# Seven block products instead of eight in one row unit of every chunk pair of w_out, gate/up and w_down

## The chip, the cores and the metric

One core of a Trainium2 chip runs the whole program in one launch. The metric is the device time of a run in microseconds (us), lower is better. The kernel before takes 2527.98 us (median of 3 runs, 2527.86 to 2528.4).

## What is computed

A decoder trunk of two layers on x of 256 positions by 2048 channels, in float32. The parts of a layer that matter here:

```python
h = rms_norm(x, mix_norm[l])
proj = h @ w_in[l]                          # q, k, v, u/v of the spatial unit, two gates
branch_a = attention(q, k, v) @ w_attn_branch[l]
branch_b = spatial_unit(u, v) @ w_sgu_branch[l]
merged = sigmoid(ga) * branch_a + sigmoid(gb) * branch_b
x = x + merged @ w_out[l]                   # 2048 x 2048
h2 = rms_norm(x, ffn_norm[l])
x = x + (silu(h2 @ w_gate[l]) * (h2 @ w_up[l])) @ w_down[l]   # FF = 5632
```

## The kernel before

All weights stream through once. A weight is cut into **chunks** of 512 columns, and a chunk into **halves** of 256 rows. `Stream` handles halves in the order of use: a DMA on SP's queue brings a half of 128x(2x512) to `raw` (L117, 512 KB, 4 buffers); ScalarE copies it to `whi` in the type fp32r (L130) and VectorE writes the rest, raw minus whi, to `wlo` (L131). Three pairs of whi and wlo exist (pool `wsp`), and `next()` asks for the split of the half that lies two ahead (`W_SPLIT` = 3), so a copy into whi waits until TensorE is done with the half three places earlier.

The activations lie transposed in **units** of 512 channels (four slices of 128), also as a high part uh and a low part ul. `product` multiplies all units with one chunk into two PSUM banks, one for each block t of 128 positions. Each half costs 2 (t) x 2 (slices of 128 rows) x 3 matmuls: uh by whi (L204), uh by wlo (L205), ul by whi (L206). That is 12 matmuls of 128x128 by 128x512 per half. After each half `tick()` issues steps that were put off with `after(n, ...)`.

In the feed-forward part each f of 11 has a gate chunk and an up chunk. After the gate product ScalarE takes tanh of both banks (L706) and VectorE multiplies (L707); after the up product VectorE finishes `hid` (L711). `transposed` then turns hid: two VectorE transposes into `box` (L218), 16 DMAs of 32 KB on SP's queue to `tt` (L222), and a split into uh and ul (L241, L242). When all 11 units of hT stand, `residual` multiplies them with the four chunks of w_down and adds each product to xs (L642); w_out goes through the same function.

TensorE's instructions run in the order in which they are written. The order on the other engines is fixed when the program is built, by a scheduler. Four PSUM banks (`ps_acc`) hold products, so two products are open at a time.

Of the kernel before, what the change touches and what calls it, by code (L numbers as in the profile page):

```python
# [8 lines left out]
F32 = mybir.dt.float32  # L9
# [5 lines left out]
P = 128  # L15
# [14 lines left out]
EPS = 1e-6  # L30
B = 32
W_LOAD = 5
W_SPLIT = 3
N_WARM = 8
TT = 1
# [12 lines left out]
def hybrid_trunk(ctx: ExitStack, tc: tile.TileContext, x, mix_norm, w_in, q_norm, k_norm, sinks,  # L48
# [16 lines left out]
    uid = [0]  # L65

    def nm(s):
        uid[0] += 1
        return f"{s}_{uid[0]}"

    def slot(shape, dt=F32, name="s"):
        return big.tile(shape, dt, tag="s4", name=nm(name))

    def temp(shape=(P, CW), name="t"):
        return tmp.tile(list(shape), F32, tag="t2", name=nm(name))

    def tiny(n, name, bufs=None):
        return small.tile([P, n], F32, tag=f"{name}{n}", name=nm(name), bufs=bufs)
# [7 lines left out]
    chunks = []  # L86
    for l in range(DEPTH):
        wl = w_in[l]
        for kind, c in FIRST_PART:
            o = {"kv": O_KV, "q": 0, "v": O_V, "u": O_U, "gate": O_GATE}[kind] + c * CW  # L90
            chunks.append(wl[:, o:o + CW])
        chunks += cols_of(w_attn_branch[l], NCH)
        for j in range(NCH):
            chunks.append(wl[:, O_GATE + D + j * CW:O_GATE + D + (j + 1) * CW])
            chunks.append(w_sgu_branch[l, :, j * CW:(j + 1) * CW])
        chunks += cols_of(w_out[l], NCH)
        for f in range(NF):
            chunks.append(w_gate[l, :, f * CW:(f + 1) * CW])
            chunks.append(w_up[l, :, f * CW:(f + 1) * CW])
        chunks += cols_of(w_down[l], NCH)  # L100
    halves = [(w, h) for w in chunks for h in range(w.shape[0] // (2 * P))]

    class Stream:

        def __init__(self):
            self.raws, self.parts = [], []
            self.at = 0

        def load(self, upto):
            while len(self.raws) < min(upto, len(halves)):
                w, h = halves[len(self.raws)]
                raw = wraw.tile([P, 2, CW], F32, tag="raw", name=nm("raw"))
                src = w[2 * h * P:2 * (h + 1) * P, :].rearrange("(k p) n -> p k n", p=P)
                if self.raws:
                    self.loaded = nc.sync.dma_start(raw, src)  # L117
                else:
                    for i in range(2):
                        self.loaded = nc.sync.dma_start(raw[:, i:i + 1], src[:, i:i + 1])  # L120
                self.raws.append(raw)

        def split(self, upto):
            while len(self.parts) < min(upto, len(halves)):
                raw = self.raws[len(self.parts)]
                hi = wsp.tile([P, 2, CW], F32R, tag="hi", name=nm("whi"))
                lo = wsp.tile([P, 2, CW], F32R, tag="lo", name=nm("wlo"))
                one = len(self.parts) < 2
                for i in ([slice(0, 1), slice(1, 2)] if one else [slice(0, 2)]):
                    nc.scalar.activation(hi[:, i, :], raw[:, i, :], AF.Copy)  # L130
                    self.last = nc.vector.tensor_tensor(out=lo[:, i, :], in0=raw[:, i, :], in1=hi[:, i, :].bitcast(F32),  # L131
                                            op=ALU.subtract)
                self.parts.append((hi, lo))
# [13 lines left out]
    def after(n, fn):  # L147
        steps.append((slot_no[0] + n, fn))
# [39 lines left out]
    def rsqrt(dst, src, n):  # L188
        nc.gpsimd.tensor_tensor(out=dst, in0=src, in1=neg_half[:, :n], op=ALU.pow)  # L189

    def product(units):

        ps = [ps_acc.tile([P, CW], F32, tag="acc", name=nm("acc")) for _ in range(NT)]
        n = 2 * len(units)
        for h in range(n):
            hi, lo = stream.next()
            uh, ul = units[h // 2]
            for t in range(NT):
                for kk in range(2):
                    k = 2 * (h % 2) + kk  # L200
                    a, b = uh[:, k, t * P:(t + 1) * P], ul[:, k, t * P:(t + 1) * P]
                    first = h == 0 and kk == 0
                    last = h == n - 1 and kk == 1
                    nc.tensor.matmul(ps[t], a, hi[:, kk, :], start=first, stop=False)  # L204
                    nc.tensor.matmul(ps[t], a, lo[:, kk, :], start=False, stop=False)  # L205
                    nc.tensor.matmul(ps[t], b, hi[:, kk, :], start=False, stop=last)  # L206
            if h < n - 1:
                tick()
        return ps

    def turn(dst, src, per=1):

# [13 lines left out]
        for j in range(4):  # L226
            after(1 + j // per, lambda j=j: move(j))

    def transposed(units, c, src, cols=None, on_pe=False):

        uh = slot([P, 4, S], F32R, "uh")
        ul = slot([P, 4, S], F32R, "ul")
# [29 lines left out]
            return  # L262

        tt = slot([P, 4, 4, NT, B], name="tt")

        def blocks_of(k0):
            return lambda k, step: tt[:, :, k0 + k:k0 + k + step].rearrange("p i k t r -> p (k t) i r")

        def done():
            parts(2, 2, blocks_of(2))  # L270
            units[c] = (uh, ul)

        turn(tt, src)
        after(6, lambda: parts(0, 2, blocks_of(0)))
        after(7, done)

    class Norm:


        def __init__(self, cols):  # L280
            self.cols = cols
            self.ss = [tiny(NCH, f"ss{t}", 2) for t in range(NT)]
            self.units = [None] * NCH

# [5 lines left out]

        def unit(self, c, on_pe=False):
            transposed(self.units, c, xs[:, :, c * CW:(c + 1) * CW], cols=self.cols[:, 4 * c:4 * c + 4],
                       on_pe=on_pe)

        def finish(self):
            self.r, self.rh, self.rr = [], [], []
# [332 lines left out]
        tick()  # L629
        return dst  # L630

    def residual(units, cols, scale=1.0):

        nxt = Norm(cols) if cols is not None else None
        for j in range(NCH):
            ps = product(units)
            for t in range(NT):
                n = 1 if cols is not None or j < NCH - 1 else 2
                w = CW // n
                for i in range(n):  # L640
                    sl = slice(j * CW + i * w, j * CW + (i + 1) * w)
                    nc.vector.scalar_tensor_tensor(out=xs[:, t, sl], in0=ps[t][:, i * w:(i + 1) * w], scalar=scale,  # L642
                                                   in1=xs[:, t, sl], op0=ALU.mult, op1=ALU.add)
                    if cols is None:
                        eng = nc.sync if i == 0 else nc.scalar
                        eng.dma_start(out[0, t * P:(t + 1) * P, sl], xs[:, t, sl])
            if cols is not None:
                after(2, lambda j=j: nxt.unit(j, j == NCH - 1))
                after(3, lambda j=j: nxt.squares(j))
                if j == NCH - 1:  # L650
                    after(4, lambda: nxt.finish())
            tick()
        return nxt

    prepare(0)
# [1 line left out]
    for l in range(DEPTH):  # L657
# [27 lines left out]
        for j in range(NCH):  # L685
            gb = gate(norm.units)
            ps = product(spa.sguT)
            for t in range(NT):
                nc.vector.scalar_tensor_tensor(out=gb[:, t, :], in0=gb[:, t, :], scalar=1.0, in1=ps[t],
                                               op0=ALU.add, op1=ALU.mult)  # L690
                nc.vector.tensor_tensor(out=ga[j][:, t, :], in0=ga[j][:, t, :], in1=gb[:, t, :], op=ALU.add)
            after(2, lambda j=j: transposed(mT, j, ga[j], on_pe=j == NCH - 1))
            tick()

        norm = residual(mT, ffn_cols(l), scale=0.5)


        if l + 1 < DEPTH:
            after(20, lambda: prepare(l + 1))
        hT = [None] * NF  # L700
        for f in range(NF):
            ps = product(norm.units)
            a = slot([P, NT, CW], name="hid")
            for t in range(NT):
                th = a[:, t, :]
                nc.scalar.activation(th, ps[t], AF.Tanh, scale=norm.rh[t])  # L706
                nc.vector.scalar_tensor_tensor(out=th, in0=th, scalar=1.0, in1=ps[t], op0=ALU.add, op1=ALU.mult)  # L707
            tick()
            ps = product(norm.units)
            for t in range(NT):  # L710
                nc.vector.scalar_tensor_tensor(out=a[:, t, :], in0=ps[t], scalar=norm.rr[t], in1=a[:, t, :],  # L711
                                               op0=ALU.mult, op1=ALU.mult)
            after(2, lambda f=f, a=a: transposed(hT, f, a))
            tick()
        norm = residual(hT, mix_cols(l + 1) if l + 1 < DEPTH else None)


# [35 lines left out]
```

## Time and profile before

| | |
|---|---|
| median of 3 runs | 2527.98 us |
| the profiled execution, its own time | 2530.42 us |
| its span, first to last instruction | 2528.7 us |
| halves, matmuls of halves | 896, 3 x 3584 |
| TensorE / VectorE / ScalarE busy | 99% / 59% / 45% |
| mean granted TensorE clock | 0.999 |

Lines of the profile name engine, source line and tile. PE is TensorE (PEld its weight loads), DVE VectorE, ACT ScalarE, SPq the DMA queue of SP. A matmul's row shows when it starts; its length of 0.39 us includes the time until its last result is out, so the next one starts before it ends.

### The profile page before, as it was taken

The page shows a single profiled execution, that of the slowest core. Times are in us where ns is not written, and L with a number is a line of the kernel's source. Part 1 is how long each engine was busy: PE and PEld are TensorE (multiplying, and loading weights), DVE is VectorE, ACT ScalarE, POOL GpSimd, SP SyncE. Part 2 cuts the span into 40 slices and gives each one's busy share as a digit, 9 for nine tenths or more (in the row PEclk, how much of TensorE's full clock was granted, in tenths as well). Part 3 has the DMA queues.
Part 4 walks back from the last instruction along what each step waited for, and adds up shares of the span by engine and source line. Part 5 has one row for each costly group of instructions (what it writes and reads, how often), then busy time and mean ns, then how long its engine had stood idle before and what let it go on. Part 6 is the DMA issues. An engine that isn't in the chain of part 4 may idle for free.

```text
span 2528.7 us, 30796 instructions
## 1 busy us (share of the span) xinstructions
PE 2515.7 (99%) x11306; PEld 2078.0 (82%) x11306; DVE 1490.8 (59%) x1817; ACT 1145.8 (45%) x1394; POOL 44.9 (2%) x51
## 2 busy tenths in 40 slices
PE   9999999999999999999999999999999999999999
PEld 7788888878888888888888888888888888888887
DVE  7786555565555555555567865556655555555444
ACT  5455444454444444444445554444444444444333
POOL 1100000000000000000000000000000000000000
PEclk9999999999999999999999999999999999999999
DMA  7656666666666666666666556666666666676665
GB/s 233 212 163 187 200 188 210 202 219 202 199 211 203 203 209 202 210 201 203 203 173 219 151 166 216 201 209 202 207 205 201 209 192 222 189 220 201 203 203 158
DMA packets 287816, 506.18 MB, mean 200 GB/s; under 512 B 28016, under 2 KB 55760, under 8 KB 287664
## 3 DMA queue, kind: packets, MB, share of 16 engines
q1 hardware_dynamic: 286544, 502.12, 64.4%
q0 software_dynamic: 800, 1.83, 0.4%
q8 instruction: 88, 1.44, 0.2%
q14 instruction: 64, 0.52, 0.1%
q10 hardware_dynamic: 320, 0.27, 0.0%
HBM read 475.27 MB, written 2.10 MB: 189 GB/s over the span
## 4 chain that ended last, share of the span: by engine, by line
PE 93%; DMA 3%; SPq 2%; DVE 1%; ACT 1%; issue 1%; POOL 0%; DVEq 0%; ACTq 0%
PE acc L205 30%; PE acc L206 30%; PE acc L204 30%; SPq L222 2%; DMA raw<-in_w_out_dram 1%; DVE wlo L131 1%; PE po L551 1%; ACT whi L130 1%; PE psc L512 1%; DMA raw<-in_w_in_dram 1%; PE ppt L541 0%; DMA raw<-in_w_down_dram 0%; DMA raw<-in_w_gate_dram 0%; PE pt L259 0%; PE psg L615 0%
## 5 line engine op out<-in xcount | busy, mean ns | idle before, releaser
L131 DVE TENSOR_TENSOR wlo<-raw,whi 128x1024 fp32r<-128x1024 f32 (+1 forms) x898 | 1094.3, 1221 | 990.2 <-ACT whi L130 982.8
L130 ACT ACTIVATE whi<-raw 128x1024 fp32r<-128x1024 f32 (+1 forms) x898 | 949.3, 1058 | 1323.2 <-PE acc L206 1078.5
L204 PE MATMUL acc<-whi,uh 128*128 128x512 f32 x3584 | 1401.2, 391 | 2.4 <-ACT whi L130 1.7
L205 PE MATMUL acc<-wlo,uh 128*128 128x512 f32 x3584 | 1396.8, 390 | 5.8 <-DVE wlo L131 5.8
L206 PE MATMUL acc<-whi,ul 128*128 128x512 f32 x3584 | 1396.0, 390 | 0.0
L205 PEld LDWEIGHTS acc<-wlo,uh 128*128 128x128 f32 x3584 | 673.3, 188 | 149.5 <-DVE wlo L131 11.2
L204 PEld LDWEIGHTS acc<-whi,uh 128*128 128x128 f32 x3584 | 673.2, 188 | 142.5 <-ACT whi L130 2.7
L206 PEld LDWEIGHTS acc<-whi,ul 128*128 128x128 f32 x3584 | 673.1, 188 | 140.0 <-DVE ul L250 0.2
L242 DVE TENSOR_TENSOR ul<-tt,uh 128x512 fp32r<-128x512 f32 x72 | 49.2, 684 | 0.0
L241 ACT ACTIVATE uh<-tt 128x512 fp32r<-128x512 f32 x72 | 40.9, 616 | 5.3 <-DMA tt<-box 5.3
L218 DVE STREAM_TRANSPOSE box<-hid 128x512 f32<-128x512 f32 x44 | 30.9, 703 | 0.0
L711 DVE SCALAR_TENSOR_TENSOR hid<-acc,rr,hid 128x512 f32<-128x512 f32 x44 | 30.9, 743 | 0.0
L529 ACT ACTIVATE pr<-pr,negm 128x128 f32<-128x128 f32 (+1 forms) x64 | 28.3, 444 | 5.3 <-DVE negm L522 5.3
L706 ACT ACTIVATE hid<-acc,rhalf 128x512 f32<-128x512 f32 x44 | 27.9, 678 | 3.2 <-PE acc L206 1.9
L707 DVE SCALAR_TENSOR_TENSOR hid<-hid,acc 128x512 f32<-128x512 f32 x44 | 28.3, 680 | 1.1 <-ACT hid L706 1.1
L551 PEld LDWEIGHTS po<-kv,pT 128*128 128x128 f32 x192 | 23.9, 191 | 1.2
L189 POOL TENSOR_TENSOR rstd<-var,neg_half 128x1 f32<-128x1 f32 x8 | 4.4, 557 | 1120.8 <-DVE var L300 1120.8
L516 DVE TENSOR_TENSOR pr<-psc,mask 128x256 f32<-128x256 f32 (+1 forms) x32 | 17.1, 550 | 11.8 <-PE psc L512 11.8
L642 DVE SCALAR_TENSOR_TENSOR xs<-acc,xs 128x512 f32<-128x512 f32 (+1 forms) x34 | 21.0, 650 | 5.1 <-PE acc L206 5.1
L628 ACT ACTIVATE gate<-acc,rhalf 128x512 f32<-128x512 f32 x32 | 21.0, 681 | 6.4 <-PE acc L206 6.4
L551 PE MATMUL po<-kv,pT 128*128 128x64 f32 x192 | 23.1, 270 | 0.0
L288 ACT ACTIVATE junk<-xs 128x512 f32<-128x512 f32 x32 | 19.9, 624 | 6.8 <-DVE xs L642 5.3
(111 smaller groups left out, 502.4 us busy)
## 6 DMA issues: line engine op xcount, KB each, us to landing
raw<-in_w_in_dram SPq DMA_DIRECT2D x239, 512.0 KB, 4.0
raw<-in_w_gate_dram SPq DMA_DIRECT2D x176, 512.0 KB, 4.3
raw<-in_w_up_dram SPq DMA_DIRECT2D x176, 512.0 KB, 4.4
raw<-in_w_down_dram SPq DMA_DIRECT2D x176, 512.0 KB, 4.2
raw<-in_w_out_dram SPq DMA_DIRECT2D x64, 512.0 KB, 4.2
tt<-box SPq DMA_DIRECT2D x784, 32.0 KB, 2.7
raw<-in_w_attn_branch_dram SPq DMA_DIRECT2D x32, 512.0 KB, 4.6
raw<-in_w_sgu_branch_dram SPq DMA_DIRECT2D x32, 512.0 KB, 4.7
```

The lines of the kernel that those rows point to most:

```text
L130: nc.scalar.activation(hi[:, i, :], raw[:, i, :], AF.Copy)
L131: self.last = nc.vector.tensor_tensor(out=lo[:, i, :], in0=raw[:, i, :], in1=hi[:, i, :].bitcast(F32), op=ALU.subtract)
L204: nc.tensor.matmul(ps[t], a, hi[:, kk, :], start=first, stop=False)
L205: nc.tensor.matmul(ps[t], a, lo[:, kk, :], start=False, stop=False)
L206: nc.tensor.matmul(ps[t], b, hi[:, kk, :], start=False, stop=last)
L218: nc.vector.transpose(box[:, :, :, t, :].rearrange("p j k r -> p k j r"), iv[:, t])
L222: nc.sync.dma_start(dst[j * B:(j + 1) * B, i], box[i * B:(i + 1) * B, j])
L241: nc.scalar.activation(h, s_, AF.Copy)
L242: nc.vector.tensor_tensor(out=l, in0=s_, in1=h.bitcast(F32), op=ALU.subtract)
L529: nc.scalar.activation(pr4[:, h, :nk], pr4[:, h, :nk], AF.Exp, bias=nm_[:, h:h + 1], accum_out=den[:, h:h + 1])
L551: nc.tensor.matmul(po[:, h, :], pT[kb][:, h, :], self.kv[:, kb, KVW + g * HD:KVW + (g + 1) * HD], start=kb == 0, stop=kb == t)
L711: nc.vector.scalar_tensor_tensor(out=a[:, t, :], in0=ps[t], scalar=norm.rr[t], in1=a[:, t, :], op0=ALU.mult, op1=ALU.mult)
```

## The change

Two chunks (w_out 0 and 1, 2 and 3; gate and up of one f; w_down likewise) become a **pair** that is multiplied together into four banks: a[0], a[1] for the first chunk, b[0], b[1] for the second. In row unit 0 of the pair (two halves of each chunk) the product of 2 position blocks by 2 halves by 2 chunks is done in seven products of 6 matmuls, in Strassen's way (Winograd's form), and not in eight. The other units are done as before, in 12 matmuls per half (tags G for the first chunk, U for the second).

```diff
-    big = ctx.enter_context(tc.tile_pool(name="big", bufs=29))
-    wraw = ctx.enter_context(tc.tile_pool(name="wraw", bufs=4))
+    big = ctx.enter_context(tc.tile_pool(name="big", bufs=24))
+    wraw = ctx.enter_context(tc.tile_pool(name="wraw", bufs=7))
...
+        return [dict(tag="P1", loads=[(k11, wa, h1)], src=k11),
+                dict(tag="P5", loads=[(k12, wb, h1)], sum=(k11, k12, k11), src=k11),
+                dict(tag="P2", loads=[(k21, wa, h2)], src=k21),
+                dict(tag="P6", loads=[(k22, wb, h2)], sum=(k11, k22, k11), src=k11),
+                dict(tag="P3", loads=[], src=k22),
+                U[0], dict(tag="P7", loads=[], sum=(k12, k22, k12), src=k12),
+                U[1], dict(tag="P4", loads=[], sum=(k21, k21, k11), src=k21)] + G + U[2:]
...
+        for f0, f1 in ROUNDS:
+            for f in range(f0, f1):
+                plans.append(pair(w_gate[l, :, f * CW:(f + 1) * CW], w_up[l, :, f * CW:(f + 1) * CW]))
+            c_ = cols_of(w_down[l, f0 * CW:f1 * CW, :], NCH)
+            plans += [pair(c_[0], c_[1]), pair(c_[2], c_[3])]
...
         def split(self, upto):
+                if e.get("sum"):
+                    d, a, b = (self.raws[key] for key in e["sum"])
+                    nc.vector.tensor_tensor(out=d, in0=a, in1=b, op=ALU.subtract)
...
+    def product_pair(units, on_a, on_b):
+        forms = {"P1": (a[1], block(units, first, 0)), "P2": (a[0], block(units, second, 0)), "P3": (b[0], s_[4]),
+                 "P4": (a[1], block(units, second, 1)), "P5": (b[0], s_[1]), "P6": (a[1], s_[2]),
+                 "P7": (a[1], s_[3])}
...
+            if tag == "P1":
+                s1 = snap("s1")
+                nc.scalar.activation(s1, a[1], AF.Copy)
+            elif tag == "P5":
+                s5 = snap("s5")
+                nc.scalar.activation(s5, b[0], AF.Copy)
+            elif tag == "P6":
+                su = snap("su")
+                nc.scalar.activation(su, a[1], AF.Copy)
+            elif tag == "P7":
+                nc.vector.tensor_tensor(out=s5, in0=a[1], in1=s5, op=ALU.add)
+            if i == last_g:
+                on_a([[a[0], s1], [a[1]]])
+            if i == len(plan) - 1:
+                on_b([[b[0], su], [b[1], s5]])
```

Each pair thus gets four subtractions of weight halves on VectorE (in place in `raw`; L158 of the changed kernel), seven splits in the place of four for its unit (hi L164, lo L165), three copies of a bank on ScalarE, an addition after P7, and evictions that add a bank and a copy (L834). The four sums on the activations' side are made once per unit 0, by `transposed(..., wino=True)`. `ROUNDS = ((0, 5), (5, 11))`: five f's, then w_down's rows that belong to them, then six f's and the rest of w_down, so xs is added to twice. There are 34 pairs: 4 for w_out, 22 for gate/up, 8 for w_down. The built program has 10548 matmuls of this kind where 10752 stood.

On VectorE before, where an up product ends and the next gate product begins (a third f of layer 0; wlo is a split's low part, hid the eviction, box a transpose):

```order
L131 TENSOR_TENSOR wlo_1055_5711<-raw_1047_5672,whi_1054_5710 128x1024
L131 TENSOR_TENSOR wlo_1058_5729<-raw_1050_5690,whi_1057_5728 128x1024
L711 SCALAR_TENSOR_TENSOR hid_1032_5591<-acc_1033_5598,rr0_894_4791,hid_1032_5591 128x512
L711 SCALAR_TENSOR_TENSOR hid_1032_5591<-acc_1034_5599,rr1_898_4800,hid_1032_5591 128x512
L131 TENSOR_TENSOR wlo_1063_5751<-raw_1053_5708,whi_1062_5750 128x1024
L218 STREAM_TRANSPOSE box_1067_5769<-hid_1032_5591 128x4x4x32
```

The same place after, from the split of P1 on (raw_1104, 1107, 1110, 1113 are k11, k12, k21, k22; the L165 rows are the splits of P1, P5, P2, P6 and P3):

```order
L165 TENSOR_TENSOR wlo_1112_5837<-raw_1104_5798,whi_1111_5836 128x1024
L158 TENSOR_TENSOR raw_1104_5798<-raw_1107_5816,raw_1104_5798 128x1024
L158 TENSOR_TENSOR raw_1107_5816<-raw_1113_5852,raw_1107_5816 128x1024
L834 TENSOR_TENSOR s5_1059_5547<-acc_1052_5521,s5_1059_5547 128x512
L165 TENSOR_TENSOR wlo_1115_5856<-raw_1104_5798,whi_1114_5855 128x1024
L834 TENSOR_TENSOR su_1069_5576<-acc_1051_5520,su_1069_5576 128x512
L847 SCALAR_TENSOR_TENSOR hid_1048_5517<-s5_1059_5547,rr1_936_4880,hid_1048_5517 128x512
L165 TENSOR_TENSOR wlo_1122_5881<-raw_1110_5834,whi_1121_5880 128x1024
L158 TENSOR_TENSOR raw_1104_5798<-raw_1113_5852,raw_1104_5798 128x1024
L847 SCALAR_TENSOR_TENSOR hid_1048_5517<-su_1069_5576,rr0_932_4871,hid_1048_5517 128x512
L158 TENSOR_TENSOR raw_1110_5834<-raw_1110_5834,raw_1104_5798 128x1024
L165 TENSOR_TENSOR wlo_1126_5896<-raw_1104_5798,whi_1125_5895 128x1024
```

Then follow a transpose (box), the splits of P3 and U[0], the second transpose and the splits of P7, U[1] and P4. Where splits followed each other with two evictions between them, ten instructions now stand between the splits of P1 and P6, and only two of them are splits; the subtraction for P4 has come ahead of the split of P6. 17 of the 22 gate/up pairs have this order row by row.

On SP's queue after, in the same pair, the loads of G halves around the 16 moves of the turned hid:

```order
L146 DMA raw_1146_5992<-in_w_gate_dram 128x2x512
L146 DMA raw_1149_6014<-in_w_gate_dram 128x2x512
L312 DMA tt_1130_5909<-box_1131_5910 32x256 x16
L146 DMA raw_1152_6026<-in_w_gate_dram 128x2x512
L146 DMA raw_1155_6044<-in_w_gate_dram 128x2x512
```

Before, the moves stood between the last loads of the next gate chunk and the first of its up chunk, with one load among them:

```order
L117 DMA raw_1128_6119<-in_w_gate_dram 128x2x512
L117 DMA raw_1131_6141<-in_w_gate_dram 128x2x512
L222 DMA tt_1123_6093<-box_1124_6094 32x256 x12
L117 DMA raw_1134_6163<-in_w_up_dram 128x2x512
L222 DMA tt_1123_6093<-box_1124_6094 32x256 x4
```

After, all 16 moves stand in one piece ahead of the fifth G half of the same pair.

More of the change, by code (lines that the diff above doesn't have):

```diff
@@ L97, in hybrid_trunk @@
[L97 to L101, printed above, removed]
+            plans.append(single(wl[:, O_GATE + D + j * CW:O_GATE + D + (j + 1) * CW]))
+            plans.append(single(w_sgu_branch[l, :, j * CW:(j + 1) * CW]))
+        c_ = cols_of(w_out[l], NCH)
+        plans += [pair(c_[0], c_[1]), pair(c_[2], c_[3])]
@@ L111, in load @@
         def load(self, upto):
[L112 to L121, printed above, removed]
@@ L191, in product @@
     def product(units):
         ps = [ps_acc.tile([P, CW], F32, tag="acc", name=nm("acc")) for _ in range(NT)]
[L194 to L197, printed above, removed]
-            for t in range(NT):
[L199 to L207, printed above, removed]
+        plan = plans[turn_of[0]]
@@ L630, in gate, with residual, chunk @@
         return dst
[L632 to L636, printed above, removed]
+    def residual(units, nxt=None, scale=1.0, store=False):
+        def chunk(j, sums):
             for t in range(NT):
-                n = 1 if cols is not None or j < NCH - 1 else 2
+                n = 2 if store and j == NCH - 1 else 1
                 w = CW // n
@@ L701, in hybrid_trunk @@
[L701 to L714, printed above, removed]
```

193 lines of the change are left out of this document (159 added, 34 removed).

## Prediction

> **What bounds the kernel now.** First the busy shares, the slices and the chain that ended last:
>
> ```profile
> PE 2515.7 (99%) x11306; PEld 2078.0 (82%) x11306; DVE 1490.8 (59%) x1817; ACT 1145.8 (45%) x1394; POOL 44.9 (2%) x51
> ...
> DVE  7786555565555555555567865556655555555444
> ...
> PEclk9999999999999999999999999999999999999999
> ...
> PE 93%; DMA 3%; SPq 2%; DVE 1%; ACT 1%; issue 1%; POOL 0%; DVEq 0%; ACTq 0%
> ```
>
> TensorE is busy in every slice at full clock and is 93% of the chain. Fewer matmuls shorten the time only if TensorE still never waits. So the groups tell what a matmul and a split cost, and whom each waits for:
>
> ```profile
> L131 DVE TENSOR_TENSOR wlo<-raw,whi 128x1024 fp32r<-128x1024 f32 (+1 forms) x898 | 1094.3, 1221 | 990.2 <-ACT whi L130 982.8
> L130 ACT ACTIVATE whi<-raw 128x1024 fp32r<-128x1024 f32 (+1 forms) x898 | 949.3, 1058 | 1323.2 <-PE acc L206 1078.5
> L205 PE MATMUL acc<-wlo,uh 128*128 128x512 f32 x3584 | 1396.8, 390 | 5.8 <-DVE wlo L131 5.8
> ```
>
> TensorE waits 5.8 us for splits in the whole run. VectorE waits 983 us for whi, and ScalarE waits 1079 us for TensorE to give a whi buffer back: the splits are paced by TensorE. The timeline shows the beat in steady state, ScalarE and VectorE:
>
> ```profile
> 714.95 1.06 ACT L130 ACTIVATE whi<-raw 128x1024 fp32r<-128x1024 f32 x1 [1.66 <-PE acc L206]
> 717.67 1.06 ACT L130 ACTIVATE whi<-raw 128x1024 fp32r<-128x1024 f32 x1 [1.66 <-PE acc L206]
> 716.04 1.23 DVE L131 TENSOR_TENSOR wlo<-raw,whi 128x1024 fp32r<-128x1024 f32 x1 [1.49 <-ACT whi L130]
> 717.24 0.39 PE L206 MATMUL acc<-whi,ul 128*128 128x512 f32 x1
> 717.47 0.39 PE L204 MATMUL acc<-whi,uh 128*128 128x512 f32 x1
> ```
>
> A half takes 717.67 - 714.95 = 2.72 us, 0.2267 a matmul. VectorE starts 0.03 us after ScalarE ends (714.95 + 1.06 = 16.01, start 16.04). The matmul of 717.24 is out at 717.63 and whi starts at 717.67: 0.2 us after that matmul's slot of 0.2267 ended. A split thus ends 2 x 2.72 - 0.2 - 1.06 - 0.03 - 1.23 = 2.9 us before TensorE turns to its half. That is the whole lead: 1.49 us of idle VectorE per half cannot be saved up, since three buffers hold the splits.
>
> **What the change removes.** 34 pairs x 6 matmuls x 0.2267 = 46.2 us of TensorE.
>
> **What it adds at a pair's beginning.** A short product lasts 6 x 0.2267 = 1.36 us, and from P1 to P3 five follow each other, each with a split of its own. VectorE's steps go by these rows:
>
> ```profile
> 704.20 1.23 DVE L131 TENSOR_TENSOR wlo<-raw,whi 128x1024 fp32r<-128x1024 f32 x1 [3.25 <-ACT whi L130]
> 705.34 0.68 DVE L242 TENSOR_TENSOR ul<-tt,uh 128x512 fp32r<-128x512 f32 x1
> 708.67 1.28 DVE L707 SCALAR_TENSOR_TENSOR hid<-hid,acc 128x512 f32<-128x512 f32 x2
> 728.06 1.40 DVE L711 SCALAR_TENSOR_TENSOR hid<-acc,rr,hid 128x512 f32<-128x512 f32 x2
> L711 DVE SCALAR_TENSOR_TENSOR hid<-acc,rr,hid 128x512 f32<-128x512 f32 x44 | 30.9, 743 | 0.0
> L218 DVE STREAM_TRANSPOSE box<-hid 128x512 f32<-128x512 f32 x44 | 30.9, 703 | 0.0
> L468 DVE TENSOR_TENSOR q<-q,sq 128x1024 f32<-128x1024 f32 x4 | 4.9, 1218 | 0.0
> 8.99 0.68 DVE L131 TENSOR_TENSOR wlo<-raw,whi 128x512 fp32r<-128x512 f32 x1
> 9.72 0.61 PE L205 MATMUL acc<-wlo,uh 128*128 128x512 f32 x1 [0.64 <-DVE wlo L131]
> ```
>
> The instruction behind a split starts 1.14 us after it (705.34 - 704.20), behind 512 elements of SBUF 0.60 (1.28 - 0.68), of PSUM 0.66 (1.40 - 0.74), behind a transpose about 0.62. The subtraction stands in no row; the nearest, two float32 inputs of the same size, takes 1.22, and I take that, plus 0.05 where the next needs its result. A waiting TensorE starts 0.05 us after VectorE ends (9.72 against 8.99 + 0.68).
>
> Now the typical gate/up pair, in VectorE's order as the change's section shows it, from T = 0, the end of the old pair's last matmul slot. The copy for P1 may start at -5.24, so its split runs from -4.15, the subtraction for P5 from -2.88, that for P7 from -1.61, s5 from -0.47. Split of P5: 0.19 to 1.42; TensorE wants it at 1.36 + 0.23 = 1.59, no wait. Then su, hid, and the split of P2 from 2.59 to 3.82: wanted at 2.72 + 0.23 = 2.95, TensorE goes on at 3.87, **0.92 late**. P2 ends 5.00. Subtraction for P6 3.73 to 4.95 (its hi follows on ScalarE to 6.06), hid, subtraction for P4 to 6.69, and the split of P6 from 6.61 to 7.84: wanted at 5.23, got at 7.89, **2.66 late**. P6 ends 9.02. A transpose, split of P3 8.37 to 9.60: wanted at 9.25, got 9.65, **0.40 late**. P3 ends 10.78; the split of U[0] is done at 10.74 and wanted at 11.0. From there halves of 2.72 us stand between the short products, and VectorE catches up. Sum 3.98 us of wait against 1.36 saved: **each such pair loses 2.62 us**.
>
> By the same steps, with each pair's own order: 18 gate/up pairs 3.98 each, 71.6. Four pairs behind a gate/up pair (first of w_down) have one addition to xs more ahead of P6's split: 4.64 each, 18.6. Five second pairs of w_down and w_out have one eviction less and mostly no transposes: 3.04 and 3.44, 16.0. The two first f's of a second round: 2.44 each, 4.9. The three pairs behind which or in which the norm's last unit is split carry eight more small VectorE steps, and their copies ahead of P6's or P5's on ScalarE: I take 6.9, 6.9 and 5.4, 19.2; without the extra steps they would have 3 each, with every step of both engines in one line 9. The two first w_out pairs carry gate evictions and a split of a unit: 5 each, 10. In all 140 us of waits, less 46: **+94 us**. If each of the seven steps between the splits of P5 and P6 took its full shown length and not its pitch, 0.07 us more per step, 0.5 per pair, it would be 17 us more.
>
> What I cost at nothing: three copies of banks on ScalarE, beside its 55% idle (s5's waits for P5, out at 2.9, and is done before P6's copy into whi may start at 5.0); the units' sums, once per unit; the second addition to xs, in halves of 2.72 us where VectorE has 1.49 idle; bank reuse, since the bank that P2 opens is read out by s5 at 0.19. The cover of each is VectorE's and ScalarE's idle time inside full halves; where it is gone, it is counted above.
>
> **The clock.** At its start the old kernel shows what TensorE's waits do; windows of 3.41 us, columns: stretch, length, busy of PE, PEld, DVE, ACT, POOL, then the granted clock:
>
> ```profile
> 3.14:6.55 3.41, 3.41 (x17) 3.15 (x16) 0.17 (x1) 1.45 (x4) 3.40 (x9) 1.00 0.92 295
> 6.55:9.96 3.41, 2.02 (x8) 0.98 (x7) 2.71 (x8) 3.40 (x9) 0.32 (x1) 1.00 1.00 333
> 9.96:13.38 3.42, 3.42 (x10) 2.54 (x10) 2.04 (x5) 1.57 (x4) 0.00 (x0) 0.50 1.00 237
> 13.38:16.79 3.41, 3.41 (x20) 2.93 (x19) 1.31 (x2) 2.40 (x6) 0.00 (x0) 1.00 1.05 399
> ```
>
> The longest idle time of the weight loads in the second stretch:
>
> ```profile
> 9.72 0.19 PEld L205 LDWEIGHTS acc<-wlo,uh 128*128 128x128 f32 x1 [1.05 <-DVE wlo L131]
> ```
>
> One stretch with 8 PE instructions and 2.02 us of busy time was followed by one at half clock, and a busy one by full clock. In my schedule a stretch of 3.41 us that starts anywhere between T = 2.3 and 6.2 holds at most 8 matmuls (from 4.0: four of P2, one of P6). Counted by the matmul slots alone, (5 x 0.2 + 0.2) of 3.41, the bound is sharper and half of all phases stay under it. So I take three of four pairs to get one stretch at half clock. It begins between 5.7 and 9.6; it stretches P6 and P3, part of which the wait for P3's split would have taken anyway: 0.2 us lost for the earliest, (13.0 - 9.65) / 2 = 1.7 for the latest, 1.0 as the middle. 0.75 x 34 x 1.0 = **25 us**; ends 0 and 57.
>
> The Trainium skill, page "TensorE: Matmul & The Clock Gate", Part 1, has the clock fall to half after a whole idle window of about 3.4 us, and its closing table asks for no idle gaps above some 3 us. The trace differs: the stretch before the fall had matmuls in it, and its longest gap was 1.05 us. By the page's rule the 25 us would not come.
>
> **Sum.** 2530.4 (the profiled execution) - 46.2 + 140 + 25 = 2649; that execution stood 2.4 us over the median, so 2647.
>
> **Rivals.**
> - *The clock stays full.* No single idle stretch of my schedule is over 1.9 us (5.00 to 6.1, one matmul, to 7.89). If such gaps don't count, 2530.4 + 94 - 2.4 = 2622. One instance in the trace speaks against it. 25%. The page's rule gives this one.
> - *TensorE never waits, and the saved matmuls come through*: 2482. It decides at the splits of P2 and P6: below 1.36 us of wait per pair the change wins. For it speaks VectorE's 41% idle; against it, that this idle time is tied to whi buffers, and that VectorE's queue holds four subtractions in line. 5%.
> - *Loads come late behind the moves.* In the new order the fifth G load stands behind 16 moves:
>
> ```profile
> 690.76 8.02 SPq L222 DMA_DIRECT2D tt<-box  x12
> raw<-in_w_gate_dram SPq DMA_DIRECT2D x176, 512.0 KB, 4.3
> ```
>
> 0.67 us a move. The second transpose ends near 11.9, the moves are issued by 22.6, the half lands at 26.9, is split at 29.2, and TensorE wants it at 30.0. With 2 us more per load, 22 pairs lose up to 2 us: 2647 + 44 = 2691. Four raw halves in hand and the clock's delay of TensorE speak against it. 10%.
>
> **How the numbers follow.** Forecast 55%; full clock 25%; late loads 10%; gain 5%; the last 5% for waits half as long as mine, near 2580 down to no change. The range reaches from the full clock with waits 15% shorter (2622 - 21, rounded to 2600) to late loads and their spread, 2700; that leaves out some 14%. A measurement of this kernel can tell about 0.2% from no change: faster 5%, same 2%, slower 93%.
>
> **What would show it.** TensorE's waits for L165 of some 140 us in all, the longest before the lo matmuls (L237) of P6, then P2, none before P5; none behind P3 but in the norm's pairs. 10548 matmuls at 0.2267 between waits. VectorE without a pause from the split of P1 to that of U[0]. A mean granted clock near 0.98 (25 stretches of 3.41 us at half in 2649); 0.999 would mean the first rival. Waits for `raw` before whi copies of the fifth G half that reach TensorE would mean the third. The forecast is wrong if VectorE's steps overlap more than their pitches say, or if the waits sit behind ScalarE.

## The result, and the profile after

The changed kernel takes **2644.19 us** (median of 4 runs, 2640.99 to 2646.69) where the kernel before took 2528.19 in the same comparison (4 runs, 2527.86 to 2528.41): ratio 1.0458, 95% interval 1.044 to 1.0476, so it is slower. The forecast was 2647. The profiled execution took 2640.99 us, with a span of 2638.9 and a mean granted clock of 0.985 (0.981 to 0.983 in the other three).

From the page of the kernel after: busy shares, two rows of slices, the chain.

```profile
PE 2533.9 (96%) x11102; PEld 2057.4 (78%) x11102; DVE 1869.2 (71%) x2229; ACT 1323.6 (50%) x1626; POOL 44.5 (2%) x51
...
DVE  7786566878776677776677865667787766776765
...
PEclk9999999999999999999999999999999999999999
...
PE 86%; DVE 9%; issue 2%; DMA 1%; ACT 1%; SPq 1%; DVEq 0%; POOLq 0%; POOL 0%; ACTq 0%
```

VectorE went from 59% to 71% busy and from 1% to 9% of the chain. Neither its share nor its slices would make one call it the bound. It is the bound only for some 10 us of each pair. The groups of the kernel after say where (busy us, mean ns of one, then idle time ahead of them and what ended it; `sh` is the activations' sum that P5, P6, P3 and P7 use):

```profile
L237 PE MATMUL acc<-wlo,sh 128*128 128x512 f32 x272 | 125.5, 461 | 45.5 <-DVE wlo L165 45.2
L237 PE MATMUL acc<-wlo,uh 128*128 128x512 f32 x3244 | 1267.0, 391 | 17.7 <-DVE wlo L165 17.7
L158 DVE TENSOR_TENSOR raw<-raw,raw 128x1024 f32<-128x1024 f32 x136 | 166.4, 1224 | 2.4
```

The 272 low-part matmuls of the short products on `sh` carry 45 us of waits, while the 3244 on `uh` have 18. A subtraction takes 1.224 us, where 1.22 was assumed. These idle times end where the matmul's row begins, and a matmul's row is longer than its slot, so they are smaller than what a wait costs; that is read from the starts. VectorE and TensorE in one typical gate/up pair, which starts (T = 0) at 995.18:

```profile
995.35 1.21 DVE L165 TENSOR_TENSOR wlo<-raw,whi 128x1024 fp32r<-128x1024 f32 x1
996.48 0.68 DVE L834 TENSOR_TENSOR su<-acc,su 128x512 f32<-128x512 f32 x1
997.08 0.74 DVE L847 SCALAR_TENSOR_TENSOR hid<-s,rr,hid 128x512 f32<-128x512 f32 x1
997.74 1.22 DVE L165 TENSOR_TENSOR wlo<-raw,whi 128x1024 fp32r<-128x1024 f32 x1
998.88 1.22 DVE L158 TENSOR_TENSOR raw<-raw,raw 128x1024 f32<-128x1024 f32 x1
1000.01 0.74 DVE L847 SCALAR_TENSOR_TENSOR hid<-su,rr,hid 128x512 f32<-128x512 f32 x1
1000.67 1.22 DVE L158 TENSOR_TENSOR raw<-raw,raw 128x1024 f32<-128x1024 f32 x1
1001.81 1.22 DVE L165 TENSOR_TENSOR wlo<-raw,whi 128x1024 fp32r<-128x1024 f32 x1
```

```profile
997.93 0.39 PE L236 MATMUL acc<-whi,uh 128*128 128x512 f32 x1
999.01 0.50 PE L237 MATMUL acc<-wlo,uh 128*128 128x512 f32 x1 [0.69 <-DVE wlo L165]
999.35 0.39 PE L238 MATMUL acc<-whi,ul 128*128 128x512 f32 x1
...
1000.05 0.39 PE L238 MATMUL acc<-whi,ul 128*128 128x512 f32 x1
1001.30 0.50 PE L236 MATMUL acc<-whi,sh 128*128 128x512 f32 x1 [0.86 <-ACT whi L164]
1003.08 0.62 PE L237 MATMUL acc<-wlo,sh 128*128 128x512 f32 x1 [1.28 <-DVE wlo L165]
1003.50 0.63 PE L238 MATMUL acc<-whi,sl 128*128 128x512 f32 x1
```

VectorE works without a pause, in the forecast's order. P2's lo matmul comes 999.01 - 997.93 - 0.2267 = 0.85 us late, and the matmul behind it another 999.35 - 999.01 - 0.2267 = 0.11. P6 starts 1.02 late, since its hi is copied from the result of the subtraction of 998.88; its lo matmul comes 1.56 later again, behind two further VectorE steps (1000.01 and 1000.67, of which the second is for P4 and not for P6). Then matmuls are 0.43 apart: the clock has been halved. The windows of this pair (as in the prediction: stretch, busy of PE, PEld, DVE, ACT, POOL, the granted clock):

```profile
996.48:999.89 3.41, 2.72 (x13) 1.88 (x12) 3.41 (x5) 1.21 (x3) 0.00 (x0) 1.00 0.00 0
999.89:1003.30 3.41, 1.27 (x5) 0.52 (x4) 3.41 (x5) 2.95 (x3) 0.00 (x0) 1.00 0.00 0
1003.30:1006.71 3.41, 3.41 (x9) 2.63 (x9) 3.21 (x4) 1.26 (x2) 0.00 (x0) 0.50 0.67 165
1006.71:1010.13 3.42, 3.42 (x16) 2.81 (x16) 2.45 (x2) 1.34 (x2) 0.00 (x0) 1.00 0.92 323
```

The page's row of clock digits shows 9 everywhere: one of its slices is 66 us long and hides 3.4 us at half. 22 of the 34 pairs have such a stretch in them, one of them two in a row. By the matmuls' starts a typical gate/up pair lasts 46.3 us without one and 47.5 with one; a pair of eight full products would last 16 x 2.72 = 43.5.

### The profile page after: what moved, and what is told of

Same layout as the page of the kernel before. It is cut to its first block, busy times and chain, and to the rows that moved or that the text cites. A ratio compares the mean times of both kernels' runs of the same rounds, so it can differ in the third digit from the quotient of the medians.

```text
span 2638.9 us, 31201 instructions
## 1 busy us (share of the span) xinstructions
PE 2533.9 (96%) x11102; PEld 2057.4 (78%) x11102; DVE 1869.2 (71%) x2229; ACT 1323.6 (50%) x1626; POOL 44.5 (2%) x51
## 4 chain that ended last, share of the span: by engine, by line
PE 86%; DVE 9%; issue 2%; DMA 1%; ACT 1%; SPq 1%; DVEq 0%; POOLq 0%; POOL 0%; ACTq 0%
PE acc L237 28%; PE acc L238 28%; PE acc L236 28%; DVE wlo L165 4%; DVE raw L158 3%; PE po L677 1%; ACT whi L164 1%; DVE hid L847 1%; SPq L312 1%; DVE su L834 1%; PE psc L638 1%; PE ppt L667 0%; DVE xs L767 0%; DMA raw<-in_w_in_dram 0%; DMA raw<-in_w_down_dram 0%
## 5 line engine op out<-in xcount | busy, mean ns | idle before, releaser
L165 DVE TENSOR_TENSOR wlo<-raw,whi 128x1024 fp32r<-128x1024 f32 (+1 forms) x1000 | 1214.0, 1219 | 704.9 <-ACT whi L164 691.5
L164 ACT ACTIVATE whi<-raw 128x1024 fp32r<-128x1024 f32 (+1 forms) x1000 | 1049.2, 1057 | 1107.5 <-PE acc L238 861.4
L237 PE MATMUL acc<-wlo,uh 128*128 128x512 f32 x3244 | 1267.0, 391 | 17.7 <-DVE wlo L165 17.7
L236 PE MATMUL acc<-whi,uh 128*128 128x512 f32 x3244 | 1270.1, 392 | 1.6 <-ACT uh L336 0.9
L238 PE MATMUL acc<-whi,ul 128*128 128x512 f32 x3244 | 1263.5, 389 | 0.0
L238 PEld LDWEIGHTS acc<-whi,ul 128*128 128x128 f32 x3244 | 609.2, 188 | 126.8 <-DVE ul L341 0.2
L237 PE MATMUL acc<-wlo,sh 128*128 128x512 f32 x272 | 125.5, 461 | 45.5 <-DVE wlo L165 45.2
L158 DVE TENSOR_TENSOR raw<-raw,raw 128x1024 f32<-128x1024 f32 x136 | 166.4, 1224 | 2.4
L236 PE MATMUL acc<-whi,sh 128*128 128x512 f32 x272 | 122.0, 448 | 29.1 <-ACT whi L164 29.1
L238 PE MATMUL acc<-whi,sl 128*128 128x512 f32 x272 | 119.9, 441 | 0.0
```

The lines of the kernel that those rows point to most:

```text
L158: nc.vector.tensor_tensor(out=d, in0=a, in1=b, op=ALU.subtract)
L236: nc.tensor.matmul(ps, a, hi[:, kk, :], start=start and kk == 0, stop=False, skip_group_check=True)
L237: nc.tensor.matmul(ps, a, lo[:, kk, :], start=False, stop=False, skip_group_check=True)
L238: nc.tensor.matmul(ps, b, hi[:, kk, :], start=False, stop=stop and kk == 1, skip_group_check=True)
```

## The experiments

Two theories at the start. *Mine*: the waits come from VectorE's line of steps between the short products, and the clock adds some 25 us. *The rival*: a wait is set by the dependence of subtraction, hi and lo of one product, or by ScalarE, and VectorE's other steps matter little. Ratios are to the kernel before, run beside each group of kernels (medians 2527.52, 2528.92 and 2528.43), with 95% intervals.

**Plain products in the new frame.** Eight full products in unit 0 too; pairs, two rounds, buffers and the activations' sums stay.

```diff
-        return [dict(tag="P1", ...), ..., dict(tag="P4", ...)] + G + U[2:]
+        return ([dict(s, tag="G") for s in single(wa)] + [dict(s, tag="U") for s in single(wb)])
...
-                on_a([[a[0], s1], [a[1]]])
+                on_a([[a[0]], [a[1]]])
             if i == len(plan) - 1:
-                on_b([[b[0], su], [b[1], s5]])
+                on_b([[b[0]], [b[1]]])
```

> Pairs, four banks, two rounds of w_down, the pools and the sums on the activations stay; the seven products of unit 0 become eight again (all halves of the first chunk, then all of the second), without subtractions and copies of banks. Theory A (waits come from VectorE's queue at the seven products): TensorE waits no more than before, 2530 to 2540 us. Rival (pairs, rounds or pools cost a good part themselves): above 2560.

Measured 2519.04, ratio 0.9964 (0.995 to 0.9978): 9 us *faster* than before, and outside what was expected. Against it the seven products cost 2644.19 - 2519.04 = 125 us, not 116.

**More raw buffers alone.** The kernel before with `wraw` 6 in the place of 4 (and `big` 27 in the place of 29); nothing else.

```diff
-    wraw = ctx.enter_context(tc.tile_pool(name="wraw", bufs=4))
+    wraw = ctx.enter_context(tc.tile_pool(name="wraw", bufs=6))
```

> The kernel before with six raw buffers in the place of four (27 big ones in the place of 29), no other change. If the plain pairs gained their 9 us by loading further ahead: 2519 to 2522 us, and the matmuls' waits near 71, 97, 387 and 528 us are gone. Rival (the gain is the pairs' and rounds'): 2527.

Measured 2519.22, ratio 0.9964 (0.995 to 0.9978). Pairs, rounds and sums therefore cost nothing measurable, and the 9 us are the raw buffers'. In the waits of the kernel before (us in total, times, longest) copies wait for loads:

```profile
ACT whi L130 <- DMA raw<-in_w_up_dram: 75.4, 34, 4.1
...
ACT whi L130 <- DMA raw<-in_w_sgu_branch_dram: 27.2, 9, 4.2
ACT whi L130 <- DMA raw<-in_w_in_dram: 25.9, 28, 5.3
...
PE acc L205 <- DVE wlo L131: 5.8, 12, 0.8
```

In those of the kernel with six raw buffers, all that is left of this kind and its TensorE row:

```profile
ACT whi L130 <- DMA raw<-in_w_in_dram: 3.0, 3, 2.0
...
PE acc L205 <- DVE wlo L131: 0.9, 2, 0.6
```

**The clock.** Eleven matmuls into a bank that nobody reads, between P2 and P6. There and inside P6 TensorE waits 1.02 + 1.56 = 2.58 us.

```diff
+            if tag == "P6":
+                fill = ps_at.tile([P, CW], F32, tag="at", name=nm("fill"))
+                for _ in range(11):
+                    nc.tensor.matmul(fill, held[0], held[1], start=True, stop=True)
...
+            if tag == "P2":
+                held = (u[0][:, 0, :], w[0][:, 0, :])
```

> As the change, with 11 idle matmuls (2.5 us) into a spare bank between P2 and P6, in the time in which TensorE waits. Clock theory (22 of 34 pairs get a stretch at half clock, 1.2 us each): the half stretches go, mean clock 0.999, 2644 - 27 = 2617 us. Rival (a stretch at half clock falls into waits and costs nothing): 2640 or more.

Measured 2618.54, ratio 1.0356 (1.0341 to 1.0372), clock 0.999: 25.7 us come back although TensorE does more. The filled kernel's page and its group of idle matmuls:

```profile
PE 2575.3 (98%) x11476; PEld 2103.5 (80%) x11476; DVE 1866.6 (71%) x2229; ACT 1329.0 (51%) x1626; POOL 45.3 (2%) x51
```

```profile
L281 PE MATMUL fill<-whi,uh 128*128 128x512 f32 x374 | 90.7, 390 | 0.0
```

So the half-clock stretches cost 26 us, and the waits are 2618.5 - (2519.0 - 46.2) = 146 us. The lengths of the pairs say the same: against matmuls at 0.2267 throughout, the 34 pairs lose 172 us in the changed kernel and 147 in the filled one, its idle matmuls counted as lost.

**Two of four subtractions on GpSimd.**

```diff
+                    eng = nc.gpsimd if e["tag"] in ("P7", "P4") else nc.vector
-                    nc.vector.tensor_tensor(out=d, in0=a, in1=b, op=ALU.subtract)
+                    eng.tensor_tensor(out=d, in0=a, in1=b, op=ALU.subtract)
```

> The subtractions for P7 and P4 on GpSimd, so two of four leave VectorE's queue ahead of P6's split. Theory A (queue and the chain subtraction, hi, lo together, by the hand schedule): waits of a gate/up pair fall from 3.98 to 2.76 us, 2644 - 41 = 2603 us, less some for fewer half-clock stretches. Rival B (only the chain from P6's subtraction over ScalarE to its split counts, not the queue): about 2640. Rival C (queue alone): waits 1.6 us, 2560.

Measured 2707.67, ratio 1.0712 (1.0696 to 1.0728), clock 0.975: 63 us worse than the changed kernel, where a gain was expected. None of the three expected times held. GpSimd and VectorE in a pair of this kernel:

```profile
1069.49 2.41 POOL L159 TENSOR_TENSOR raw<-raw,raw 128x1024 f32<-128x1024 f32 x1 [39.20 <-DVE raw L159]
1076.58 2.75 POOL L159 TENSOR_TENSOR raw<-raw,raw 128x1024 f32<-128x1024 f32 x1 [4.68 <-DVE raw L159]
```

```profile
1069.73 0.69 DVE L835 TENSOR_TENSOR s<-acc,s 128x512 f32<-128x512 f32 x1 [0.46 <-PE acc L239]
1070.46 1.99 DVE L848 SCALAR_TENSOR_TENSOR hid<-s,rr,hid 128x512 f32<-128x512 f32 x1
...
1077.63 2.79 DVE L166 TENSOR_TENSOR wlo<-raw,whi 128x1024 fp32r<-128x1024 f32 x1 [0.52 <-ACT whi L165]
```

GpSimd subtracts from 1069.49 to 1071.90. VectorE's s, with one input from PSUM, runs beside it in its usual 0.69. Its hid, with two inputs from SBUF, needs 1.99 in the place of 0.74 and ends 0.55 after GpSimd does; the next wlo, begun while GpSimd works from 1076.58 to 1079.33, needs 2.79 and ends 1.09 after that. Both look as if they start only when GpSimd is done. The Trainium skill, page "SBUF — State Buffer", section "Who interferes with whom", says that a VectorE instruction with two inputs from SBUF contends with a GpSimd instruction that reads SBUF, and that the shared ports are an exclusive lock: the second one is blocked, not slowed. The trace agrees in all three VectorE rows. So the subtractions left VectorE's count and stayed in its time: in this pair P5's lo matmul starts 1.16 us late, where it wasn't late before, and P6's 2.60 in the place of 1.56.

**The same two subtractions left out.** The short products P7 and P4 then multiply halves that were not subtracted, so this kernel's result is not the product; TensorE, ScalarE and the loads do the same work.

```diff
-                if e.get("sum"):
+                if e.get("sum") and e["tag"] not in ("P7", "P4"):
```

> The change without the subtractions for P7 and P4 (their products take the halves as they are, so the sums are wrong); all else as it was. Theory A (VectorE's queue and the chain subtraction, hi, lo, by the hand schedule): a gate/up pair waits 2.8 us and not 4.0; half-clock stretches get fewer; 2595 to 2605 us. Rival B (only the chain behind P6's subtraction): 2640. Rival C (queue alone, 2.4 us less): 2560.

Measured 2583.48, ratio 1.0219 (1.0204 to 1.0234). 61 us go, 12 more than at the lower end of the 2595 to 2605 expected, though neither subtraction is needed by the products that wait longest (P2 and P6). Part of the 61 is the clock: 10 half-clock stretches are left of 23. A typical pair without a half-clock stretch goes from 46.3 to 45.13 us: P2's wait falls from 0.85 to 0.24, P6's lo from 1.56 to 1.03, P6's hi stays at 1.02. The time lies between the 2560 of a queue alone and the 2640 of a chain alone. Both theories have a part: VectorE's line sets how late P2 and P6's lo are, and P6's hi and the last 1.03 of its lo are the chain of its own subtraction, hi and lo (a lo that starts when its hi is out comes 1.22 + 0.05 - 0.2267 = 1.04 after the time it is wanted).

**A lead of four splits.** `W_SPLIT` 4, four pairs of whi and wlo, `wraw` 6 and `big` 23 to make room.

```diff
-W_SPLIT = 3
+W_SPLIT = 4
-    wsp = ctx.enter_context(tc.tile_pool(name="wsp", bufs=3))
+    wsp = ctx.enter_context(tc.tile_pool(name="wsp", bufs=4))
```

> The change with four buffers for splits in the place of three (W_SPLIT 4; paid for with one raw and one big buffer): splits may run 2.72 us further ahead. Theory A: of 4.0 us of wait per pair about 0.7 is left, at P3, and no half-clock stretches: 2519 - 46 + 34 x 0.7 + some 15 in the norm's pairs = 2512 us. Rival (VectorE cannot keep up at the pair's beginning however early it may start): 2600 or more.

Measured 2541.71, ratio 1.0051 (1.0036 to 1.0066). Typical gate/up pairs last 43.1 to 44.0 us: some 0.8 us of wait is left at P3's lo matmul, where 0.7 was put. So the mechanism held, yet the time is 30 us over the 2512 expected. Part of that are four pairs of 46.8 to 47.8 us, the third f of each round. The first reading, on which the next expectation rests, was that the load of the fourth half comes late there. The trace doesn't show it: neither VectorE nor ScalarE waits for a load in the last 12 us before these pairs or in the first 12 of them. What differs is VectorE's order: the split of the activations' sums stands ahead of the pair, and three or four evictions stand ahead of P6's subtraction, where typical pairs have none.

**Lead of four, seven raw buffers**, and four temporaries for five, three copies of banks for four:

```diff
-    wraw = ctx.enter_context(tc.tile_pool(name="wraw", bufs=6))
-    tmp = ctx.enter_context(tc.tile_pool(name="tmp", bufs=5))
+    wraw = ctx.enter_context(tc.tile_pool(name="wraw", bufs=7))
+    tmp = ctx.enter_context(tc.tile_pool(name="tmp", bufs=4))
```

> The order of the changed kernel with a lead of four splits, as in the run that took 2541.7, but with seven raw halves in the place of six. There typical pairs took 43.2 to 43.75 us and some 47, where the load of the fourth half came late. If the sixth buffer was what made it late, the long pairs go to 43.5: 2515 to 2525. If something else made them long (the moves of the turned hid, the copies on ScalarE), it stays at 2535 to 2545.

Measured 2524.91, ratio 0.9988 (0.9978 to 0.9997): 17 us better, at the upper end of the 2515 to 2525 expected. 14 of the gate/up pairs last 43.1. Three of the four long ones come to 43.8 to 44.3, the fourth stays at 47.8. VectorE's order in the three is another one again, so it is not shown that the missing buffer had made them long. Seven products are now level with the old kernel, though still 6 us behind plain products with six raw buffers.

**Short products spread out.** In 28 pairs a full half stands between one short product and the next (P1, P5, U0, P2, U1, P6, U2, P3, U3, P7, G0, P4); a subtraction may not overtake the split ahead of it. The four pairs of w_out and the first f of each layer stay.

```diff
-                    nc.vector.tensor_tensor(out=d, in0=a, in1=b, op=ALU.subtract)
+                    with tc.issue_after(self.last.ins):
+                        nc.vector.tensor_tensor(out=d, in0=a, in1=b, op=ALU.subtract)
```

> A half of U or G between the short products (in 28 of 34 pairs), each subtraction held behind the split of the entry before it. Theory A: VectorE has 2.7 us more per short product, only P5's split is still late, by 1.1 us, since su and hid stand ahead of it; 2530 - 46 + 28 x 1.1 + some 30 for the six pairs left as they are = 2545 us. Rival (VectorE's added work is too much wherever it stands): above 2600.

Measured 2576.49, ratio 1.019 (1.0173 to 1.0207), clock 0.999: 68 us better than the change, 31 us short of the expectation. With a lead of three P5's split is still 1.15 us late, as expected, and smaller waits come to it: a typical gate/up pair lasts 44.84, 2.7 over the 42.16 without waits. The first f of a second round, behind w_down, lasts 42.5. The two first f's that stay lose 8.6 and 8.7 us, where they lost 5.6 and 6.4.

**Spread out, with a lead of four**, four pairs of whi and wlo and six raw buffers:

```diff
-W_SPLIT = 3
+W_SPLIT = 4
-    wraw = ctx.enter_context(tc.tile_pool(name="wraw", bufs=7))
+    wraw = ctx.enter_context(tc.tile_pool(name="wraw", bufs=6))
```

> Both: halves between the short products in 28 of 34 pairs, and four buffers for splits. Theory A: no wait in those 28 pairs, some 30 us in the six that are left as they are; 2519 - 46 + 30 = 2503 us, faster than before. Rival (loads come late with six raw buffers, or VectorE is full): 2530 or more.

Measured 2649.28, ratio 1.0477 (1.0461 to 1.0492), clock 0.981. The expected time was missed by 146 us, and the rival that it named came true. The waits of this kernel:

```profile
ACT whi L173 <- DMA raw<-in_w_gate_dram: 114.1, 21, 7.7
PEld acc L245 <- ACT whi L173: 83.7, 27, 4.6
```

In the spread order k11 to k22 stay in `raw` for much of the pair, so only two of six buffers are left for loads, and the G halves are issued behind the 16 moves of the turned hid. Two runs take these causes apart.

**Spread, lead of four, seven raw buffers**, with four temporaries for five and three copies of banks for four:

```diff
-    wraw = ctx.enter_context(tc.tile_pool(name="wraw", bufs=6))
+    wraw = ctx.enter_context(tc.tile_pool(name="wraw", bufs=7))
```

> The spread order with a lead of four splits once more, with seven raw halves in the place of six and everything else as it was there (three copies of banks and one temporary less, to make room). In the run with six, four of them were held by the halves that the subtractions share, and the waits for a G half's load reached TensorE with some 4 us per gate/up pair (2649). If the held buffers are what makes these loads late, a seventh lets the loads run one further ahead and most of that is gone: 27 pairs x 4 = 108 less, some 2540, and 2500 if nothing else is late. If the 16 moves of the turned hid in front of the G loads on SP's queue are what makes them late, the seventh buffer gives little: 2600 or more.

Measured 2575.67, ratio 1.0183 (1.0165 to 1.0202): 74 us of the 146, between the 2540 of the one cause and the 2600 of the other. **The same with the moves spaced out:** groups of four moves two halves apart, with G loads between them, and the split of the turned hid four halves later.

```diff
-            after(1 + j // per, lambda j=j: move(j))
+            after(1 + gap * (j // per), lambda j=j: move(j))
```

> The kernel of the run with seven raw halves and spread short products, with the 16 moves of a turned hid issued in groups of four at every second half and not of four at every half, and the split of the turned hid four halves later (not for the last hid of a round), so that G loads stand between the groups on SP's queue. If the moves make the G loads late, this one gets them in time: 2519 (plain products with more raw buffers) - 46 for the matmuls + some 20 to 30 us in the norm's and w_out's pairs, which keep their order or their waits = 2495 to 2510, faster than before. If the held buffers make them late, it goes as the run with seven buffers and the moves in one piece.

Measured **2534.05**, ratio 1.002 (1.0011 to 1.003): 42 us more. SP's queue with the moves in one piece, then with the moves spaced:

```profile
1038.79 10.54 SPq L321 DMA_DIRECT2D tt<-box  x16
1049.43 2.58 SPq L154 DMA_DIRECT2D raw<-in_w_gate_dram  x5
```

```profile
1021.32 4.95 SPq L321 DMA_DIRECT2D tt<-box  x8
1026.36 0.53 SPq L154 DMA_DIRECT2D raw<-in_w_gate_dram  x1
1026.93 2.41 SPq L321 DMA_DIRECT2D tt<-box  x4
1029.44 1.09 SPq L154 DMA_DIRECT2D raw<-in_w_gate_dram  x2
1030.58 2.92 SPq L321 DMA_DIRECT2D tt<-box  x4
```

In one piece the moves keep the queue for 10.5 us, four halves' worth of TensorE, and five G loads stand behind them. Spaced, 19 of the 34 pairs (16 of gate/up, three of w_down) lose nothing: 42.16 us a gate/up pair, 43.52 less the whole 1.36. One of them in the windows of that kernel, TensorE busy throughout:

```profile
1012.50:1054.60 42.10, 42.10 (x187) 34.90 (x186) 34.37 (x36) 23.41 (x26) 0.00 (x0) 1.00 0.61 212
```

The other 15 pairs (w_out's, the norm's, the third f of a round, and the first ones of w_down, ahead of which the moves stay in one piece) lose up to 7.1 us each and eat the gain: they were put at 20 to 30 us and come to 2534 - (2519 - 46) = 61, so the expected 2495 to 2510 was missed.

**Short products two by two**, with a lead of four, seven raw buffers and the moves in one piece; the plan of the spread order becomes (loads and sums left out):

```diff
-P1, P5, U[0], P2, U[1], P6, U[2], P3, U[3], P7, G[0], P4, G[1:], U[4:]
+P1, P5, U[0], P2, P6, U[1], P3, P7, U[2], P4, G, U[3:]
```

> Lead of four splits, seven raw halves, and a U half behind P5, P6 and P7, so that short products follow each other two by two. VectorE then has two splits and two subtractions per 5.4 us, 4.8 us of work without the evictions. If TensorE's waits in the changed kernel come from VectorE's line of steps, some 1 us per pair is left: 2519 - 46 + 34 + 20 in the norm's pairs = 2525; if G loads are late as in the spread order, 2560 or more.

Measured 2573.94, ratio 1.0175 (1.0159 to 1.0191). A typical gate/up pair waits 1.03 us at P7 and 0.5 at P4, and up to 1.7 at the G halves that come behind the moves: both expected losses at once, and the time is that of the second (2560 or more).

The fastest kernels here are those with plain products and more raw buffers, at 2519. Seven products in only those pairs that lose nothing by them, plain ones in the rest, would come to about 2519 - 19 x 1.36 = 2493, an estimate from these rows; it wasn't tried.

## Why the prediction was right, step by step

- **Matmuls removed, 46.2 us**: right. A pair without waits lasts 42.16 us, 43.52 - 1.36.
- **VectorE's line of steps**: right in mechanism, place and size. In the typical pair P5 doesn't wait; P2's lo matmul starts at T = 3.83 (forecast 3.87), P6's hi at 6.12 (6.1), its lo at 7.90 (7.89). The third late split, P3's, was put at 0.40 and shows 0.24. In all 3.67 us against 3.98. That pitches and not shown lengths count is confirmed with it.
- **The other pairs**: by waits of over 0.25 us, first pairs of w_down show 4.03 (forecast 4.64), second ones 2.5 (3.04), a first f of a second round 2.05 (2.44). The norm's three pairs show 4.1 to 4.9 us (5.4 to 6.9). The first pairs of w_out lose 3.07 us at one place, as was roughly the size put down (5), for another cause: TensorE's own transposes of the gated unit wait for VectorE's gate, not for a split. By these sums most pairs were put a little too high, and yet all waits together are 146 us against 140. The rest is in small steps: behind a late lo matmul the next one starts another 0.11 us late, as at 999.35, some three times a pair. By their whole lengths, pairs without a half-clock stretch lose 46.3 - 42.16 = 4.1 us (typical, forecast 3.98), 4.7 (first of w_down), 3.0 (second) and 2.5 (first f of a second round): the forecast, within 0.2. Why the next matmul starts late, no run here shows. One sign of the forecast failed: P5 does wait in a few pairs, longest in the third f of the first layer (1.53 us).
- **The clock**: right, as the filler run shows. 22 pairs in the place of 25.5, 1.2 us each in the place of 1.0, 26 us in the place of 25. Fewer stretches at a higher price: that these cancel is luck. The first rival, by which the clock stays full because no single idle gap is long enough, is out: the typical pairs' gaps are at most 1.6 us, and their clock falls.
- **TensorE never waits** (2482): out for this order of work, yet real for another. With short products spread out, a lead of four and the moves spaced, it happens in 19 pairs.
- **Loads late behind the moves**: out for the changed kernel, whose waits of whi copies for gate halves are few and shorter than the lead of a split (2.9 us):

```profile
ACT whi L164 <- DMA raw<-in_w_gate_dram: 9.1, 11, 1.6
```

  In the spread order with six raw buffers loads do come late. Of the 146 us lost there, a seventh buffer gave back 74 and the spacing of the moves 42, near the 44 that this rival was given for another order.
- **What failed** is the start of the sum. It takes all of the old kernel's 2530 as TensorE's work and leaves out three more raw buffers, which the diff shows. The old kernel's slices were all 9 and TensorE's waits on splits 5.8 us, but loads reached TensorE with some 9 us. That error (-9) and those of the waits (+6) and the clock (+1) nearly cancel: 2647 - 9 + 6 + 1 = 2645, measured 2644. Since errors of opposite sign cancel, the match to 0.1% is luck; the steps were good to some 9 us.

## What to carry to other kernels

Where one engine is full and others feed it, count the feeders' work per piece of the full engine's work, at the shortest pieces: here 71% busy on average, and no slack at all for 10 us of each pair. Fewer instructions on the full engine pay only if each short piece is preceded by enough long ones; order and depth of the lead decided between +125 us and almost nothing with the same arithmetic. Try the plain kernel in the new frame first: here buffers that came along with the change were worth more than the change.

## What the runs showed of the hardware that was not expected

**The clock falls after a stretch that is mostly idle, though not wholly.** Stretches of 3.413 us follow each other without regard to the work (half-clock ones start at 955.51 and 1003.30, 14 x 3.413 apart, where the pairs start 47.38 apart). With each matmul's start counted as a slot of 0.2267 us, all 22 stretches of the changed kernel ahead of a half-clock one (the first 20 us left out) leave TensorE at least 2.16 us idle (1 to 6 matmuls begin in them), and none that leaves at most 2.07 idle is followed by one. The middle one of three neighbouring stretches of another pair wasn't followed by a fall:

```profile
692.69:696.10 3.41, 2.72 (x13) 1.87 (x11) 3.41 (x5) 2.07 (x3) 0.00 (x0) 1.00 0.00 0
696.10:699.51 3.41, 1.91 (x6) 1.03 (x6) 3.41 (x4) 2.25 (x3) 0.00 (x0) 1.00 0.00 0
699.51:702.93 3.42, 2.71 (x11) 1.92 (x12) 3.42 (x5) 2.01 (x3) 0.00 (x0) 1.00 0.44 129
```

In the other runs the two kinds mix between about 2.0 and 2.2 us idle, with one fall after 1.6 in a pair with transposes. So some 60% idle was enough here. Read as a wholly idle window, the Trainium skill's rule (page "TensorE: Matmul & The Clock Gate", Part 1, table of the two states: after at least one idle window) is too mild for this kernel. The forecast's bound of at most 8 matmuls was too wide. Its sharper one, 1.2 us of slots in 3.41, is 2.2 us idle and near what was measured; the forecast took a share of pairs between the two.

**GpSimd is no free helper for float32 subtractions.** One of 128x1024 takes 2.54 us on average (2.41 and 2.75 in the rows above) against VectorE's 1.22, and in these rows VectorE's instructions with two inputs from SBUF that come meanwhile are held up. Moving 68 of them took 166.4 - 82.8 = 84 us of subtractions from VectorE and lengthened its splits by 60 us and its hid by 36.
